# The FFN's up projection with high and low activations as one 512-column operand

## The chip, the cores and the metric

One core of a Trainium2 chip runs the kernel. The metric is the device time of one execution in microseconds (us), the median of several runs. Names: PE is TensorE's matmuls, PEld its weight loads, DVE is VectorE, ACT is ScalarE, POOL is GpSimd, SP is SyncE.

## What is computed

One decoder layer on 256 tokens of width 2048, in float32: a hybrid mixer, a cross-attention into 256 memory tokens, and an FFN, each with an RMSNorm before and after and a residual sum. The part that matters here is the FFN (width 5632, so 11,264 columns in the up projection), whose conv runs over the tokens:

```python
def conv_ffn(h, w_up, conv_w, conv_b, w_down):
    s = h.shape[1]
    up = h @ w_up
    up_pad = jnp.pad(up, ((0, 0), (CONV_WIDTH - 1, 0), (0, 0)))
    conv = conv_b + sum(up_pad[:, j:j + s] * conv_w[j] for j in range(CONV_WIDTH))
    gate, val = jnp.split(conv, 2, axis=-1)
    return (jax.nn.gelu(gate, approximate=True) * val) @ w_down
```

## The kernel before

Every large product is made of three: operands are split into a high part (rounded to `fp32r`) and a low part (the rest), and high x high, high x low and low x high are summed in PSUM. Weights come from memory in units of 512 KB (`raw_load`, line 204, four buffers), ScalarE casts the high half (line 220) and VectorE subtracts it from the raw weights for the low half (line 222), each with three buffers (`split`, line 214).

In `wstat` (line 241) the weights are the stationary operand and the activations stream as 256 columns, one for each token. A call makes 256 output columns, that is two weight tiles of 128 (`t`), in two PSUM tiles `mm` of which only the first 256 of 512 columns are used; four such tiles turn. Its 16 k-tiles come as four units of four. For each unit and each `t` there are 12 matmuls: high weights with high and low activations alternately for four k-tiles (lines 252 and 254), then the low weights with the high activations for the four (line 257). Each matmul loads its weights anew. In `xstat` the activations are stationary and the weights stream as 512 columns (lines 277, 279, 283); the down projection uses that.

The FFN runs 22 steps of two `wstat` calls, gate columns and value columns (lines 1392 and 1397), 44 calls and 88 weight tiles in all. Behind a call, `conv` (line 1380) takes each of the two PSUM tiles: VectorE multiplies by the tokens' norm factor `x2row` (1382) into `z`, ScalarE makes the first conv term with the bias (1383), VectorE adds the two shifted terms (1384, 1386). Behind the gate there is a GELU (1395); behind the value the product of both (1400) and its split into `hid` (1403, 1404), which waits in SBUF for the down projection.

The activations `h3T` are made by `transposed` (line 333): PE transposes, ScalarE casts the high part, VectorE makes the low part (line 329). A `Packed` holder keeps a tile with the high parts of two k-tiles and another with their low parts. All 16 buffers `h` are taken by it; they come free during the last call, when the last gains are loaded into four of them from GpSimd's queue.

A scheduler sets the order of each engine's instructions from priorities. Casts and differences of the split are issued with a high priority (`AHEAD`), so that they stand ahead of the conv of calls that come earlier in the program text; on an engine instructions run in the order in which they stand.

Of the kernel before, what the change touches and what calls it, by code (L numbers as in the profile page):

```python
# [61 lines left out]
class Packed:  # L62


    def __init__(self, per):
        self.per = per
        self.hi = []
        self.lo = []
# [3 lines left out]

    def l(self, k):
        return self.lo[k // self.per][:, k % self.per, :]


class Concat:
# [82 lines left out]
def hybrid_block(tc, a, out, dbg=None):  # L160
    nc = tc.nc
    dbg = dbg or {}
    with ExitStack() as ctx:
# [17 lines left out]
        def view(t_, **kw):  # L181
            keys = " ".join(kw)
            return t_.rearrange(f"p ({keys}) -> p {keys}", **kw)
# [57 lines left out]
        def wstat(src, c0, nco, X, kts=None):  # L241
# [17 lines left out]
                    L.advance(UNIT * n / 8)  # L259
            return [p[:, :S] for p in ps]  # L260

        def xstat(src, kts, c0, nco, X, ps, first=True, last=True, tail=1):


            nk = len(kts)
            hold = []
            for k0, n, hv, lv in units(src, kts, c0, nco):
                hold.append((k0, n, hv, lv))
                if nk - tail * n <= k0 and k0 + n < nk:
                    continue  # L270
                for t in range(2):
                    ts_ = slice(t * P, (t + 1) * P)
                    o = ps[t][:, :nco]
                    for k0, n, hv, lv in hold:
                        for k in range(n):
                            kk = kts[k0 + k]
                            nc.tensor.matmul(o, lhsT=X.h(kk)[:, ts_], rhs=hv[:, k, :],  # L277
                                             start=(first and k0 + k == 0), stop=False)
                            nc.tensor.matmul(o, lhsT=X.l(kk)[:, ts_], rhs=hv[:, k, :],  # L279
                                             start=False, stop=False)  # L280
                        for k in range(n):
                            kk = kts[k0 + k]
                            L.last = nc.tensor.matmul(o, lhsT=X.h(kk)[:, ts_], rhs=lv[:, k, :],  # L283
                                                      start=False, stop=(last and k0 + k == nk - 1))
                        L.advance(UNIT * n * nco / 2048)
                hold = []
# [43 lines left out]
                                               op1=ALU.subtract)  # L330
            return r

        def transposed(X, src, gcol, new):


            for j in range(KT // 2):
                ps = (auxp, auxq)[j % 2]()
                pv = view(ps, k=2, t=S)
                for t in range(2):
                    for k in range(2):  # L340
                        f = (2 * j + k) * P
                        nc.tensor.transpose(pv[:, k, t * P:(t + 1) * P],
                                            src[t][f // 512][:, f % 512:f % 512 + P], ident)
                hi = view(new(), k=2, t=S)
                lo = view(new(), k=2, t=S)
                for k in range(2):
                    X.last = put_hi_lo(hi[:, k, :], lo[:, k, :], pv[:, k, :], scale=gcol(2 * j + k))
                X.hi.append(hi)
                X.lo.append(lo)
                yield 1.5  # L350

        def row_factors(src, tmp, pins=(None,) * 4):
# [66 lines left out]
        def gcol(n):  # L419
            return lambda k: gpar[:, n * KT + k:n * KT + k + 1]  # L420
# [944 lines left out]
                    nc.sync.dma_start(dbg["x2"][t * P:(t + 1) * P, c * 512:(c + 1) * 512], x2[t][c])  # L1365


        h3T = Packed(2)
        with tc.high_priority(offset=2 * AHEAD):
            for _ in transposed(h3T, x2, gcol(2), hbuf):  # L1370
                pass
        x2row = over_rows(row_factors(x2, xtmp))
        right2.close()
# [5 lines left out]

        def conv(ps, dst, n):  # L1380
            z = mk(fp, "z", 4, (P, S))
            nc.vector.tensor_tensor(z, ps, x2row, op=ALU.mult)  # L1382
            nc.scalar.activation(dst, z, AF.Identity, bias=cw[:, 3, n:n + 1], scale=cw[:, 2, n:n + 1])  # L1383
            nc.vector.scalar_tensor_tensor(dst[:, 1:], z[:, :S - 1], cw[:, 1, n:n + 1], dst[:, 1:],  # L1384
                                           op0=ALU.mult, op1=ALU.add)
            nc.vector.scalar_tensor_tensor(dst[:, 2:], z[:, :S - 2], cw[:, 0, n:n + 1], dst[:, 2:],
                                           op0=ALU.mult, op1=ALU.add)

        hid = Packed(2)
        for j in range(FT // 2):  # L1390
            g = mk(fp, "gv", 4)
            ps = wstat(w_up, j * 256, 256, h3T)
            for t in range(2):
                conv(ps[t], g[:, t * S:(t + 1) * S], 2 * j + t)
            nc.scalar.activation(g, g, AF.Gelu_apprx_tanh)
            v = mk(fp, "gv", 4)
            ps = wstat(w_up, D_FF + j * 256, 256, h3T)
            for t in range(2):
                conv(ps[t], v[:, t * S:(t + 1) * S], FT + 2 * j + t)
            nc.vector.tensor_tensor(v, v, g, op=ALU.mult)  # L1400
            hi = mk(fp, "hid", FT, dt=F32R)
            lo = mk(fp, "hid", FT, dt=F32R)
            nc.scalar.copy(hi, v)
            nc.vector.tensor_tensor(lo, v, hi.bitcast(F32), op=ALU.subtract)
            hid.hi.append(view(hi, k=2, t=S))
            hid.lo.append(view(lo, k=2, t=S))
# [35 lines left out]
```

## Time and profile before

| | us |
|---|---|
| median of 3 runs | 1379.72 (1379.4 to 1380.31) |
| the profiled execution | 1382.32 |
| its span, first to last instruction | 1380.6 |
| PE busy | 1346.1 |
| PEld busy | 1250.1 |
| DVE busy | 867.5 |
| ACT busy | 685.1 |
| POOL busy | 78.7 |

The span is what the profile's views cover. The up projection lies at about 618 to 1132 us in it, the down projection behind that to about 1371 us. Ends of matmuls are modelled, and one begins while the one before it drains; so the distance of starts tells the pace, and the mean duration does not.

### The profile page before, as it was taken

Reading aid. Unit: us, or ns where it says so; the run is one execution under the profiler, and the core shown is the slowest. Engines: PE = TensorE matmul, PEld = TensorE weight load, DVE = VectorE, ACT = ScalarE, POOL = GpSimd, SP = SyncE. Lnnn points to the kernel's source line nnn. Section 1 sums busy time; section 2 is a strip of 40 time slices with the busy share of each in tenths; the row PEclk is TensorE's granted clock in tenths of the full one; section 3 lists DMA queues with packets and bytes.
Section 4 is the critical chain, followed back from the end, with each engine's and each line's share of the span. In section 5 each row is a group of like instructions: output and inputs, shape, how many; then the busy total and the mean of one; then the engine's idle time right before and its main releaser. Section 6 shows DMA issues by size and latency. Waiting matters only on the chain.

```text
span 1380.6 us, 23271 instructions
## 1 busy us (share of the span) xinstructions
PE 1346.1 (97%) x9412; PEld 1250.1 (91%) x9412; DVE 867.5 (63%) x1277; ACT 685.1 (50%) x1011; POOL 78.7 (6%) x99
## 2 busy tenths in 40 slices
PE   6999999999999999989999999999999999999997
PEld 6889989989988879869999999999999998888886
DVE  5679954456565765576666666666666674444444
ACT  6755372244456655566555555555555553434342
POOL 3011001120003110010000000000000000000001
PEclk9999999999999999999999999999999999999998
DMA  7545553145548755444655565555565566666663
GB/s 231 157 124 168 146 168 90 49 154 152 151 140 288 249 164 172 157 130 147 187 179 184 182 187 179 186 180 187 180 186 180 187 210 197 194 193 194 194 193 130
DMA packets 189849, 238.97 MB, mean 173 GB/s; under 512 B 7920, under 2 KB 144013, under 8 KB 189741
## 3 DMA queue, kind: packets, MB, share of 16 engines
q1 hardware_dynamic: 185802, 225.76, 53.0%
q0 software_dynamic: 3376, 11.29, 2.5%
q8 instruction: 74, 1.21, 0.4%
q10 hardware_dynamic: 563, 0.43, 0.1%
q14 instruction: 34, 0.28, 0.1%
HBM read 235.33 MB, written 2.12 MB: 172 GB/s over the span
## 4 chain that ended last, share of the span: by engine, by line
issue 57%; PE 37%; DVE 2%; POOL 1%; DMA 1%; ACT 1%; ACTq 0%; DVEq 0%; POOLq 0%
PE mm L252 5%; PE mm L257 5%; PE mm L254 5%; PE mm L277 4%; PE mm L279 4%; PE mm L283 4%; PE auxq L625 1%; DMA wa<-in_rwkv_w_up_dram 1%; PE auxq L742 1%; PE auxp L742 1%; DVE lo L222 1%; DMA raw<-in_w_in_dram 0%; PE auxq L864 0%; PE auxp L921 0%; PE auxp L892 0%
## 5 line engine op out<-in xcount | busy, mean ns | idle before, releaser
L222 DVE TENSOR_TENSOR lo<-raw,hi 128x1024 fp32r<-128x1024 f32 x422 | 516.6, 1225 | 373.5 <-ACT hi L220 372.1
L220 ACT CAST hi<-raw 128x1024 fp32r<-128x1024 f32 x422 | 441.8, 1048 | 459.1 <-PE mm L254 251.4
L252 PE MATMUL mm<-h,hi 128*128 128x256 f32 x2000 | 507.8, 286 | 1.6 <-ACT h L328 1.6
L254 PE MATMUL mm<-h,hi 128*128 128x256 f32 x2000 | 504.9, 285 | 0.3 <-DVE h L329 0.3
L252 PEld LDWEIGHTS mm<-h,hi 128*128 128x128 f32 x2000 | 385.2, 193 | 3.7 <-ACT h L328 1.8
L254 PEld LDWEIGHTS mm<-h,hi 128*128 128x128 f32 x2000 | 384.8, 193 | 1.3 <-DVE h L329 0.6
L257 PE MATMUL mm<-h,lo 128*128 128x256 f32 x2000 | 324.6, 284 | 0.0
L257 PEld LDWEIGHTS mm<-h,lo 128*128 128x128 f32 x2000 | 277.6, 193 | 1.2 <-issue 1.0
L279 PE MATMUL mm<-hi,hid 128*128 128x512 f32 x352 | 136.9, 389 | 0.0
L277 PE MATMUL mm<-hi,hid 128*128 128x512 f32 x352 | 136.9, 389 | 0.0
L283 PE MATMUL mm<-lo,hid 128*128 128x512 f32 x352 | 108.3, 389 | 0.0
L1383 ACT ACTIVATE gv<-z,cw 128x256 f32<-128x256 f32 x88 | 53.0, 602 | 71.6 <-DVE z L1382 71.6
L277 PE MATMUL mm<-hi,h 128*128 128x512 f32 (+1 forms) x208 | 78.9, 385 | 0.7 <-ACT hi L220 0.7
L277 PEld LDWEIGHTS mm<-hi,hid 128*128 128x128 f32 x352 | 66.1, 188 | 13.8
L283 PEld LDWEIGHTS mm<-lo,hid 128*128 128x128 f32 x352 | 66.1, 188 | 13.7
L279 PEld LDWEIGHTS mm<-hi,hid 128*128 128x128 f32 x352 | 66.0, 188 | 13.6
L279 PE MATMUL mm<-hi,h 128*128 128x512 f32 (+1 forms) x208 | 77.0, 375 | 0.0
L1384 DVE SCALAR_TENSOR_TENSOR gv<-z,cw,gv 128x255 f32<-128x255 f32 x88 | 42.3, 481 | 29.5 <-ACT gv L1383 29.5
L283 PE MATMUL mm<-lo,h 128*128 128x512 f32 (+1 forms) x208 | 59.6, 374 | 0.2 <-DVE lo L222 0.2
L277 PEld LDWEIGHTS mm<-hi,h 128*128 128x128 f32 x208 | 39.2, 188 | 8.1 <-ACT hi L220 1.1
L279 PEld LDWEIGHTS mm<-hi,h 128*128 128x128 f32 x208 | 39.2, 189 | 6.2
L283 PEld LDWEIGHTS mm<-lo,h 128*128 128x128 f32 x208 | 37.3, 188 | 7.7 <-DVE lo L222 0.8
(329 smaller groups left out, 1280.4 us busy)
## 6 DMA issues: line engine op xcount, KB each, us to landing
raw<-in_ffn_w_up_dram SPq DMA_DIRECT2D x176, 512.0 KB, 3.6
raw<-in_w_in_dram SPq DMA_DIRECT2D x94, 512.0 KB, 4.4
raw<-in_ffn_w_down_dram SPq DMA_DIRECT2D x88, 512.0 KB, 4.9
raw<-in_w_out_dram SPq DMA_DIRECT2D x32, 512.0 KB, 3.9
raw<-in_mem_wkv_dram SPq DMA_DIRECT2D x16, 512.0 KB, 4.2
raw<-in_mem_wq_dram SPq DMA_DIRECT2D x8, 512.0 KB, 3.6
raw<-in_mem_wo_dram SPq DMA_DIRECT2D x8, 512.0 KB, 3.7
x<-in_x_dram SPq DMA_DIRECT2D x8, 256.0 KB, 6.5
```

Of the source, the lines that this page charges most:

```text
L220: nc.scalar.copy(hv, rv)
L222: nc.vector.tensor_tensor(lv, rv, hv.bitcast(F32), op=ALU.subtract)
L252: nc.tensor.matmul(o, lhsT=hv[:, k, cs], rhs=X.h(k0 + k), start=(k0 + k == 0), stop=False)
L254: nc.tensor.matmul(o, lhsT=hv[:, k, cs], rhs=X.l(k0 + k), start=False, stop=False)
L257: L.last = nc.tensor.matmul(o, lhsT=lv[:, k, cs], rhs=X.h(k0 + k), start=False, stop=(k0 + k == nk - 1))
L277: nc.tensor.matmul(o, lhsT=X.h(kk)[:, ts_], rhs=hv[:, k, :], start=(first and k0 + k == 0), stop=False)
L279: nc.tensor.matmul(o, lhsT=X.l(kk)[:, ts_], rhs=hv[:, k, :], start=False, stop=False)
L283: L.last = nc.tensor.matmul(o, lhsT=X.h(kk)[:, ts_], rhs=lv[:, k, :], start=False, stop=(last and k0 + k == nk - 1))
L625: nc.tensor.matmul(ps[e][:, n * P:(n + 1) * P], lhsT=l[pr, t0:t0 + P], rhs=r[pr, t0:t0 + P], start=True, stop=True)
L742: nc.tensor.matmul(pv[:, n, c0:], lhsT=BN[:, g * 4 + n, :], rhs=G[g][:, n, c0:], start=True, stop=True)
L1383: nc.scalar.activation(dst, z, AF.Identity, bias=cw[:, 3, n:n + 1], scale=cw[:, 2, n:n + 1])
L1384: nc.vector.scalar_tensor_tensor(dst[:, 1:], z[:, :S - 1], cw[:, 1, n:n + 1], dst[:, 1:], op0=ALU.mult, op1=ALU.add)
```

## The change

The activations of the FFN lie in a new holder, `Paired`: for each k-tile one tile, whose first 256 columns are the high and whose last 256 are the low part. A new function, `wstat2`, makes one matmul of 512 columns with the high weights against that whole tile, into all 512 columns of the PSUM tile: the first half collects high x high, the second high x low. Directly behind it comes the matmul of the low weights with the 256 high columns, into the second half. `conv` then has two halves to add: ScalarE copies the second half to SBUF, VectorE adds the first half to it, and GpSimd multiplies by `x2row`. The first gate call keeps `wstat`; the other 43 calls use `wstat2`.

```diff
+class Paired:
+    def __init__(self):
+        self.hl = []
+    def h(self, k):
+        return self.hl[k][:, 0, :]
+    def l(self, k):
+        return self.hl[k][:, 1, :]
...
+        def wstat2(src, c0, nco, X):
+            nt = nco // P
+            ps = [mmps() for _ in range(nt)]
+            for k0, n, hv, lv in units(src, list(range(KT)), c0, nco):
+                for t in range(nt):
+                    cs = slice(t * P, (t + 1) * P)
+                    for k in range(n):
+                        nc.tensor.matmul(view(ps[t], z=2, t=S), lhsT=hv[:, k, cs], rhs=X.hl[k0 + k],
+                                         start=(k0 + k == 0), stop=False)
+                        L.last = nc.tensor.matmul(ps[t][:, S:], lhsT=lv[:, k, cs], rhs=X.h(k0 + k),
+                                                  start=False, stop=(k0 + k == KT - 1))
+                    L.advance(UNIT * n / 8)
+            return ps
...
-                hi = view(new(), k=2, t=S)
-                lo = view(new(), k=2, t=S)
+                one, two = view(new(), k=2, t=S), view(new(), k=2, t=S)
                 for k in range(2):
-                    X.last = put_hi_lo(hi[:, k, :], lo[:, k, :], pv[:, k, :], scale=gcol(2 * j + k))
...
+                    hi, lo = ((one, two)[k][:, i, :] if paired else (one, two)[i][:, k, :] for i in range(2))
+                    X.last = put_hi_lo(hi, lo, pv[:, k, :], scale=gcol(2 * j + k))
+                if paired:
+                    X.hl += [one, two]
...
-        h3T = Packed(2)
+        h3T = Paired()
...
         def conv(ps, dst, n):
             z = mk(fp, "z", 4, (P, S))
-            nc.vector.tensor_tensor(z, ps, x2row, op=ALU.mult)
+            if ps.shape[1] == S:
+                nc.vector.tensor_tensor(z, ps, x2row, op=ALU.mult)
+            else:
+                nc.scalar.copy(z, ps[:, S:])
+                nc.vector.tensor_tensor(z, ps[:, :S], z, op=ALU.add)
+                nc.gpsimd.tensor_tensor(z, z, x2row, op=ALU.mult)
...
-            ps = wstat(w_up, j * 256, 256, h3T)
+            ps = (wstat2 if j else wstat)(w_up, j * 256, 256, h3T)
...
-            ps = wstat(w_up, D_FF + j * 256, 256, h3T)
+            ps = wstat2(w_up, D_FF + j * 256, 256, h3T)
```

The order on PE, for one unit and one weight tile in the middle of the up projection (`mm` is the PSUM tile, `h` activations, `hi` and `lo` the weights' halves; a number is a buffer's own). Before:

```order
L252 MATMUL mm_9934<-h_6326,hi_9998 128x256
L254 MATMUL mm_9934<-h_6327,hi_9998 128x256
L252 MATMUL mm_9934<-h_6326,hi_9998 128x256
L254 MATMUL mm_9934<-h_6327,hi_9998 128x256
L252 MATMUL mm_9934<-h_6337,hi_9998 128x256
L254 MATMUL mm_9934<-h_6338,hi_9998 128x256
L252 MATMUL mm_9934<-h_6337,hi_9998 128x256
L254 MATMUL mm_9934<-h_6338,hi_9998 128x256
L257 MATMUL mm_9934<-h_6326,lo_9999 128x256 x2
L257 MATMUL mm_9934<-h_6337,lo_9999 128x256 x2
```

and with the change:

```order
L284 MATMUL mm_8044<-h_6326,hi_8092 128x512
L286 MATMUL mm_8044<-h_6326,lo_8093 128x256
L284 MATMUL mm_8044<-h_6327,hi_8092 128x512
L286 MATMUL mm_8044<-h_6327,lo_8093 128x256
L284 MATMUL mm_8044<-h_6337,hi_8092 128x512
L286 MATMUL mm_8044<-h_6337,lo_8093 128x256
L284 MATMUL mm_8044<-h_6338,hi_8092 128x512
L286 MATMUL mm_8044<-h_6338,lo_8093 128x256
```

Twelve matmuls of 256 columns are now eight, four of 512 and four of 256, and the low weights come second instead of ninth.

The order on ACT behind a value call. Before:

```order
L1383 ACTIVATE gv_8979<-z_9102,cw 128x256
L220 CAST hi_9182<-raw_9180 128x1024
L1383 ACTIVATE gv_8979<-z_9107,cw 128x256
L220 CAST hi_9212<-raw_9210 128x1024
L1403 CAST hid_9113<-gv_8979 128x512
L220 CAST hi_9256<-raw_9254 128x1024
L220 CAST hi_9286<-raw_9284 128x1024
```

and with the change:

```order
L1417 COPY z_8134<-mm_8044 128x256
L233 CAST hi_8202<-raw_8200 128x1024
L1420 ACTIVATE gv_8043<-z_8134,cw 128x256
L1417 COPY z_8141<-mm_8045 128x256
L233 CAST hi_8224<-raw_8222 128x1024
L1420 ACTIVATE gv_8043<-z_8141,cw 128x256
L233 CAST hi_8264<-raw_8262 128x1024
L1440 CAST hid_8149<-gv_8043 128x512
L233 CAST hi_8286<-raw_8284 128x1024
```

A copy of the low half stands ahead of each `gv` step, the first of them ahead of the cast that was behind the step.

The order on DVE behind a value call, from its first `z` to the next call's. Before:

```order
L1382 TENSOR_TENSOR z_9646<-mm_9524,rrow_6390 128x256
L1384 SCALAR_TENSOR_TENSOR gv_9523<-z_9646,cw,gv_9523 128x255
L1382 TENSOR_TENSOR z_9651<-mm_9525,rrow_6390 128x256
L1386 SCALAR_TENSOR_TENSOR gv_9523<-z_9646,cw,gv_9523 128x254
L222 TENSOR_TENSOR lo_9727<-raw_9724,hi_9726 128x1024
L1384 SCALAR_TENSOR_TENSOR gv_9523<-z_9651,cw,gv_9523 128x255
L1386 SCALAR_TENSOR_TENSOR gv_9523<-z_9651,cw,gv_9523 128x254
L1400 TENSOR_TENSOR gv_9523<-gv_9523,gv_9389 128x512
L222 TENSOR_TENSOR lo_9757<-raw_9754,hi_9756 128x1024
L1404 TENSOR_TENSOR hid_9658<-gv_9523,hid_9657 128x512
L222 TENSOR_TENSOR lo_9801<-raw_9798,hi_9800 128x1024
```

and with the change:

```order
L1418 TENSOR_TENSOR z_8134<-mm_8044,z_8134 128x256
L235 TENSOR_TENSOR lo_8203<-raw_8200,hi_8202 128x1024
L1421 SCALAR_TENSOR_TENSOR gv_8043<-z_8134,cw,gv_8043 128x255
L1418 TENSOR_TENSOR z_8141<-mm_8045,z_8141 128x256
L1423 SCALAR_TENSOR_TENSOR gv_8043<-z_8134,cw,gv_8043 128x254
L235 TENSOR_TENSOR lo_8225<-raw_8222,hi_8224 128x1024
L1421 SCALAR_TENSOR_TENSOR gv_8043<-z_8141,cw,gv_8043 128x255
L1423 SCALAR_TENSOR_TENSOR gv_8043<-z_8141,cw,gv_8043 128x254
L1437 TENSOR_TENSOR gv_8043<-gv_8043,gv_7937 128x512
L235 TENSOR_TENSOR lo_8265<-raw_8262,hi_8264 128x1024
L1441 TENSOR_TENSOR hid_8150<-gv_8043,hid_8149 128x512
L235 TENSOR_TENSOR lo_8287<-raw_8284,hi_8286 128x1024
```

The sum of the two halves stands where the product by the norm factor stood; the first low difference, which stood behind two shifted conv terms, now stands ahead of them.

## Rows read from the trace of the kernel before

**Rows 1.** The page, parts 1 and 2: busy time, share of the span and instructions of each engine, and the granted TensorE clock in 40 slices, in tenths.

```profile
PE 1346.1 (97%) x9412; PEld 1250.1 (91%) x9412; DVE 867.5 (63%) x1277; ACT 685.1 (50%) x1011; POOL 78.7 (6%) x99
...
PEclk9999999999999999999999999999999999999998
```

**Rows 2.** Busy time by stretches (us from the span's start): the start of the up projection, its middle, and the down projection. Columns: stretch, length, busy us (count) of PE, PEld, DVE, ACT and POOL, granted clock, share of the DMA engines, GB/s.

```profile
620.00:630.00 10.00, 9.69 (x60) 9.42 (x60) 7.36 (x16) 8.35 (x24) 0.00 (x0) 0.69 0.17 54
660.00:1120.00 460.00, 460.00 (x3835) 460.00 (x3835) 313.19 (x440) 231.56 (x279) 0.00 (x0) 1.00 0.59 184
1150.00:1300.00 150.00, 150.00 (x663) 124.21 (x662) 70.36 (x60) 60.56 (x63) 0.00 (x0) 1.00 0.63 193
```

**Rows 3.** The waits from 690 to 1130 us, the two longest that lie in the way of the splits: who waited for whom, us in total, times, longest.

```profile
ACT hi L220 <- PE mm L254: 145.6, 114, 1.8
DVE lo L222 <- ACT hi L220: 115.9, 97, 1.7
```

**Rows 4.** The instructions of line 257, the low weights' matmul, from 654.85 to 1130.05 us: count, duration in ns (least, median, most), first and last start.

```profile
L257 PE MATMUL mm<-h,lo x1320: 283/283/284, 654.9 to 1129.0; 128*128 128x256 f32 x189
```

**Rows 5.** The timeline of PE, the first burst of that count and the first one behind it: start in us, us from the first start to the last end, engine, line, operation, how many.

```profile
654.90 0.64 PE L257 MATMUL mm<-h,lo 128*128 128x256 f32 x4
...
1130.10 0.64 PE L257 MATMUL mm<-h,lo 128*128 128x256 f32 x4
```

**Rows 6.** The timeline of PE in the down projection, columns as in the group before.

```profile
1201.41 0.39 PE L277 MATMUL mm<-hi,hid 128*128 128x512 f32 x1
1201.63 0.39 PE L279 MATMUL mm<-hi,hid 128*128 128x512 f32 x1
1201.86 0.39 PE L277 MATMUL mm<-hi,hid 128*128 128x512 f32 x1
1202.09 0.39 PE L279 MATMUL mm<-hi,hid 128*128 128x512 f32 x1
1202.31 0.61 PE L283 MATMUL mm<-lo,hid 128*128 128x512 f32 x2
1202.77 0.39 PE L277 MATMUL mm<-hi,hid 128*128 128x512 f32 x1
```

**Rows 7.** The timeline of PE at the two passages between sizes: from the mixer's gate (512 columns) to its next projection (256), and from the up to the down projection.

```profile
325.80 0.62 PE L283 MATMUL mm<-lo,h 128*128 128x512 f32 x2
326.25 0.28 PE L252 MATMUL mm<-h,hi 128*128 128x256 f32 x1
...
1131.54 0.64 PE L257 MATMUL mm<-h,lo 128*128 128x256 f32 x4
1132.02 0.40 PE L277 MATMUL mm<-hi,hid 128*128 128x512 f32 x1
```

**Rows 8.** The timeline around the end of one unit of the up projection; in brackets the idle time before and what ended it.

```profile
806.10 0.64 PE L257 MATMUL mm<-h,lo 128*128 128x256 f32 x4
806.30 1.05 ACT L220 CAST hi<-raw 128x1024 fp32r<-128x1024 f32 x1 [1.83 <-PE mm L254]
807.38 1.23 DVE L222 TENSOR_TENSOR lo<-raw,hi 128x1024 fp32r<-128x1024 f32 x1 [1.65 <-ACT hi L220]
```

**Rows 9.** Instructions by line and shape, 690 to 1130 us: line, engine, operation, out<-in, count, busy us, mean ns of one, idle time before them and what ended it.

```profile
L222 DVE TENSOR_TENSOR lo<-raw,hi 128x1024 fp32r<-128x1024 f32 x154 | 188.3, 1223 | 115.9 <-ACT hi L220 115.9
L220 ACT CAST hi<-raw 128x1024 fp32r<-128x1024 f32 x153 | 159.8, 1044 | 147.0 <-PE mm L254 145.6 <-PE mm L257 1.3
L1383 ACT ACTIVATE gv<-z,cw 128x256 f32<-128x256 f32 x76 | 45.7, 602 | 61.8 <-DVE z L1382 61.8
L1384 DVE SCALAR_TENSOR_TENSOR gv<-z,cw,gv 128x255 f32<-128x255 f32 x76 | 36.5, 481 | 25.4 <-ACT gv L1383 25.4
L1386 DVE SCALAR_TENSOR_TENSOR gv<-z,cw,gv 128x254 f32<-128x254 f32 x76 | 36.4, 479 | 1.3
L1382 DVE TENSOR_TENSOR z<-mm,rrow 128x256 f32<-128x256 f32 x76 | 31.7, 417 | 0.0
L1400 DVE TENSOR_TENSOR gv<-gv,gv 128x512 f32<-128x512 f32 x19 | 13.2, 693 | 0.7
L1404 DVE TENSOR_TENSOR hid<-gv,hid 128x512 fp32r<-128x512 f32 x19 | 13.0, 684 | 0.0
```

**Rows 10.** The instructions of line 867, a ScalarE copy from PSUM in the mixer; columns as in rows 4.

```profile
L867 ACT COPY s<-auxq x6: 372/372/378, 246.1 to 278.6; 128x256 f32<-128x256 f32 x6
```

**Rows 11.** What GpSimd and VectorE do beside each other elsewhere, by the views of single lines; columns as in rows 4. Lines 1264 and 1266 are the two halves of a residual sum and run at the same time.

```profile
L806 POOL TENSOR_TENSOR nat<-nat,wa x3: 1346/1349/1446, 136.2 to 175.6; 128x512 f32<-128x512 f32 x3
...
L1264 POOL TENSOR_TENSOR yg<-yg,row x2: 1758/1759/1760, 503.1 to 511.0; 128x512 f32<-128x512 f32 x2
...
L1266 DVE SCALAR_TENSOR_TENSOR yg<-yg,small,row x6: 743/751/1773, 502.3 to 511.5; 128x512 f32<-128x512 f32 x6
...
L436 POOL MEMSET cmask<- x1: 312/312/312, 0.9 to 0.9; 128x256 f32 x1
...
L568 POOL MEMSET v<- x1: 527/527/527, 41.5 to 41.5; 128x516 f32 x1
```

**Rows 12.** The page, part 6: the up projection's loads, KB each, median us from issue to landing.

```profile
raw<-in_ffn_w_up_dram SPq DMA_DIRECT2D x176, 512.0 KB, 3.6
```

**Rows 13.** The timeline of PE at the start of the up projection.

```profile
616.66 0.69 PE L342 MATMUL auxp<-ident,row 128*128 128x128 f32 x2 [3.40 <-DVE row L1266]
618.28 0.78 PE L252 MATMUL mm<-h,hi 128*128 128x256 f32 x2
```

More of the change, by code (lines that the diff above doesn't have):

```diff
@@ L331, in put_hi_lo, with transposed @@
             return r
-        def transposed(X, src, gcol, new):
+        def transposed(X, src, gcol, new, paired=False):
             for j in range(KT // 2):
@@ L343, in transposed @@
                                             src[t][f // 512][:, f % 512:f % 512 + P], ident)
-                hi = view(new(), k=2, t=S)
-                lo = view(new(), k=2, t=S)
+                one, two = view(new(), k=2, t=S), view(new(), k=2, t=S)
                 for k in range(2):
-                    X.last = put_hi_lo(hi[:, k, :], lo[:, k, :], pv[:, k, :], scale=gcol(2 * j + k))
-                X.hi.append(hi)
-                X.lo.append(lo)
+                    hi, lo = ((one, two)[k][:, i, :] if paired else (one, two)[i][:, k, :] for i in range(2))
[3 more added lines that the diff above has]
+                else:
+                    X.hi.append(one)
+                    X.lo.append(two)
                 yield 1.5
@@ L1365, in hybrid_block @@
                     nc.sync.dma_start(dbg["x2"][t * P:(t + 1) * P, c * 512:(c + 1) * 512], x2[t][c])
-        h3T = Packed(2)
+        h3T = Paired()
         with tc.high_priority(offset=2 * AHEAD):
-            for _ in transposed(h3T, x2, gcol(2), hbuf):
+            for _ in transposed(h3T, x2, gcol(2), hbuf, paired=True):
                 pass
@@ L1381, in conv @@
             z = mk(fp, "z", 4, (P, S))
-            nc.vector.tensor_tensor(z, ps, x2row, op=ALU.mult)
+            if ps.shape[1] == S:
+                nc.vector.tensor_tensor(z, ps, x2row, op=ALU.mult)
+            else:
+                nc.scalar.copy(z, ps[:, S:])
+                nc.vector.tensor_tensor(z, ps[:, :S], z, op=ALU.add)
+                nc.gpsimd.tensor_tensor(z, z, x2row, op=ALU.mult)
             nc.scalar.activation(dst, z, AF.Identity, bias=cw[:, 3, n:n + 1], scale=cw[:, 2, n:n + 1])
```

## The prediction

> **What bounds the kernel now.** I read the busy shares first. TensorE is busy 97% of the span, VectorE 63%, ScalarE 50%, GpSimd 6%, and the granted clock is full in nearly every slice [rows 1]. A busy PE is no proof of a bound, because its ends are modelled, so I read the stage by stretches next: through the up projection (660 to 1120 us) PE and its weight loads are busy without a gap, VectorE is busy 313 of 460 us, ScalarE 232, GpSimd 0, and the clock is 1.00 [rows 2]. The waits say the same from the other side: ScalarE's high casts wait for PE 114 times, VectorE's low differences wait for ScalarE 97 times, and of this stage no wait of PE stands in the list [rows 3]. So PE's issue pace sets the time of this stage, and the splits run up to three buffers ahead of it.
>
> The pace comes from starts, not from durations. From the low burst at 654.90 us to the one at 1130.10 us [rows 5] lie 1,320 low matmuls, four to a burst [rows 4], so 330 bursts of 12 matmuls: 475.20 / 330 = 1.440 us a burst, **120.0 ns for a matmul of 256 columns**, its weight load included. In the down projection six matmuls of 512 columns start between 1201.41 and 1202.77 us [rows 6]: **226.7 ns each**. Their difference, 106.7 ns, is 256 columns at 2.4 GHz; what is left of both, 13.3 ns, is a cost per matmul that does not grow with its columns. That is what the change can save.
>
> **The change part by part.** *Matmuls.* For one k-tile and one weight tile there were three matmuls of 256 columns, 3 x 120.0 = 360.0 ns; now one of 512 and one of 256, 226.7 + 120.0 = 346.7 ns. 13.3 ns go. 43 of the 44 calls are changed (the diff leaves the first as it was), each with 2 weight tiles and 16 k-tiles: 1,376 pairs, 1,376 x 13.33 ns = **18.3 us**. The streamed columns stay 768. Sizes mixed in one stream are not in the trace in steady state, but both passages are: the last 256-column matmul of a burst of four at 1131.54 us and the first of 512 behind it lie 120 ns apart (1131.54 + 4 x 0.12 = 1132.02), and two 512-column matmuls from 325.80 us with a 256-column one behind them at 326.25 us take 0.225 us each [rows 7]. Neither passage pays extra. Bounds: nothing saved, if the mixed stream kept 360 ns, and 26.7 ns a pair (36.7 us), if a second fixed cost also vanished. I take 13.3, which is where both passages lie. Is the clock in danger when columns are denser? The down projection, with 512 of every 544 cycles used, holds 1.00 [rows 2].
>
> The rows say 13.3 ns of fixed cost per matmul. The Trainium skill, page "TensorE: Matmul & The Clock Gate", section "Back-to-back issue gap", gives about 2.5 ns beside the columns when the clock is full; by that, 1,376 matmuls fewer would be worth an estimated 3.4 us, and the median would come to 1376.3 us. For the sum the measurement decides; what could keep the cost where it is stands among the rivals.
>
> *Low weights earlier.* A unit of four k-tiles used its low half a third of the way in; now at its second matmul. And high buffers, released at 20 of 24 matmuls before (the cast at 806.30 us starts while the last low burst from 806.10 us still runs, and the low difference follows at 807.38 us for 1.23 us [rows 8]), now come free only at the end. Three buffers turn, so the low half is needed two units after the release, 2 x 2.77 = 5.5 us, and costs a cast, 1.05, and a difference, 1.22 [rows 9]: some 3.2 us to spare when nothing stands between.
>
> *The conversion behind a call.* Before: one product from PSUM (0.42 us), the ScalarE step (0.60), two VectorE steps (0.48 each) [rows 9]. Now: a ScalarE copy from PSUM, 0.37 us by the nearest row [rows 10]; a VectorE sum from PSUM and SBUF, the old product's shape, 0.42; a GpSimd product of 128x256, which has no row. GpSimd's 128x512 tensor-tensor takes 1.35 us at the median of one line and 1.76 in another, where VectorE works beside it [rows 11], so 0.67 to 0.88 if it goes by columns, and 1.76 at most; I take 0.7 to 0.9, since its memsets do go by columns (0.31 us for 256, 0.53 for 516 [rows 11]). Per pair of calls VectorE is busy 8 x 1.22 + 4 x (0.42 + 0.48 + 0.48) + 0.69 + 0.68 = 16.7 us [rows 9], the same as before, of now 64 x 0.3467 = 22.2 us. ScalarE gets 4 x 0.37 us more.
>
> Does the longer chain hold back a split? I walk the order shown, from T, where PE ends a call's first tile. Copy to T+0.4, sum to 0.8, product to 1.6. The unit ends at 1.4: cast to 2.4, ScalarE step to 3.0, second copy to 3.4. VectorE: low difference 2.4 to 3.7, step to 4.1, second sum to 4.6, step to 5.0. The second product, held by that step, runs 5.0 to 5.8. ScalarE: cast at the next release, 4.2 to 5.2, step 5.8 to 6.4, free before the release at 6.9. VectorE may wait for GpSimd until 5.8: low difference to 7.0, two steps and the product of the halves to 8.6, low difference to 9.9, and so on to 12.0, after which the next call's sum follows without a backlog. The four low halves are ready at 3.7, 7.0, 9.9 and 12.0 and needed at 6.9, 9.7, 12.5 and 15.2: **at least 2.6 us to spare**. All of it lies beside PE and costs nothing; without that cover the copy and the product alone, 0.37 + 0.8 us for each of 86 tiles, would be 100 us.
>
> *Queues.* SP's order of loads is unchanged. Loads of 512 KB land in 3.6 us [rows 12]; 184 GB/s becomes 191, below the 193 the down projection draws without a gap [rows 2]. On GpSimd two gain loads now stand ahead of one product in the second last call; they wait for the first buffers of the last call, free at about T+3.5, and that product's input is ready at T+4.6. The PSUM tiles are released by VectorE's sum at T+4.6 instead of T+2, a call of 11.1 us before they are needed.
>
> *The start.* The up projection runs from 618.28 us to 1132.02 us [rows 7, 13], 513.7 us against 44 calls x 8 bursts x 1.44 = 506.9: it loses 6.9 us while activations are transposed and the clock is down to 0.69 [rows 2]. The pairs change in which tile a high and a low part lie, and with it the order there. Twelve matmuls, one burst, is the size by which that order moves: -1.5 to +2 us; I take 0.
>
> **Sum.** 18.3 us. The profiled execution took 1382.3 us (span 1380.6), 2.6 over the median 1379.7; all of it falls off the span: 1382.3 - 18.3 = 1364.0 for such an execution, 1379.7 - 18.3 = **1361.4 us** for the median.
>
> **The rivals.** *A lock (slower).* GpSimd and VectorE hold each other up: the VectorE step of 128x512 beside GpSimd's sum has a median of 751 ns and a maximum of 1773, and GpSimd's sum grows from 1.35 to 1.76 [rows 11]. Each of the four products in two calls takes VectorE's time if it blocks it whole, and VectorE becomes the bound from (22.2 - 16.7) / 4 = 1.37 us each on; a queue that is in order would suffer somewhat earlier. At 1.76 us: 16.7 + 7.0 = 23.7 us for two calls instead of 23.0 before, 21.5 times: +15 us, 1395 us. Against it: half the columns. 0.05. (The Trainium skill, page "SBUF — State Buffer", section "Who interferes with whom", states such an exclusive lock for a VectorE instruction with two SBUF inputs, which the low difference is; the maximum above agrees.)
>
> *Part of it eaten.* Products near 1.1 us make the step behind them late for some casts, or the start loses more than 2 us: 3 to 13 us faster, 1367 to 1377 us. 0.08.
>
> *The cost stays.* If the 13 ns go with the columns or with how closely a short matmul follows its weights, and not with the number of matmuls, a pair of unlike lengths keeps its 360 ns: no change, 1380 us. Against it: proportional to columns, 512 would take 240 ns and not 226.7, and both passages. 0.04. (The Trainium skill's figure above lies beside this case.) *A new wait of the same size*, a few tenths of a microsecond at each call's end, 18.3 / 43 = 0.43 us: 1380 us as well. Against it: 2.6 us to spare. 0.02.
>
> **How the numbers follow.** The forecast, 1359 to 1367 us, has 0.81. The range is that: 18.3 us with the start (-1.5 to +2) and 0.9 us of spread of the runs shown at the fast end, and 3.6 us of lost casts at the slow end; past it lies 0.19. About 0.2% (2.8 us) can be told from no change: faster 0.81 + 0.08 = 0.89, same 0.04 + 0.02 = 0.06, slower 0.05.
>
> **What would show it.** The two matmuls of a pair starting 0.347 us apart from the next pair; PE still without a gap between 660 us and the stage's end, which moves from 1132 to about 1114; VectorE's busy time nearly unchanged; 86 products on GpSimd of 0.7 to 0.9 us. It is wrong if PE waits for VectorE's low difference, if products take over 1.1 us, or if pairs stand more than 0.35 us apart.

## The result

The changed kernel takes 1373.83 us (median of 13 runs, 1371.59 to 1379.02), the kernel before 1380.98 us in the same comparison (13 runs, 1379.33 to 1384.02): a ratio of 0.9946, 95% interval 0.9936 to 0.9957. On the 1379.72 us shown above that is 1372.3 us. It is faster, by 7.4 us (5.9 to 8.8), where 18.3 us were forecast; the time lies above the range.

The profiled execution took 1375.61 us, its span is 1373.9 us. The page, parts 1 and 2, answers to [rows 1]:

```profile
PE 1337.0 (97%) x8036; PEld 1175.1 (86%) x8036; DVE 869.4 (63%) x1277; ACT 715.7 (52%) x1097; POOL 149.6 (11%) x185
...
PEclk9999999999999999999999999999999999999999
```

1,376 matmuls are gone (9,412 to 8,036), GpSimd has 86 instructions more, and VectorE's busy time is the old one. The stretches of [rows 2], columns as there:

```profile
660.00:1120.00 460.00, 460.00 (x2605) 398.95 (x2604) 320.13 (x449) 264.67 (x368) 69.60 (x86) 1.00 0.60 187
1150.00:1300.00 150.00, 150.00 (x663) 124.23 (x662) 69.95 (x59) 60.97 (x64) 0.00 (x0) 1.00 0.61 193
```

PE still has no gap, the clock is still 1.00, the loads draw 187 GB/s, fewer than the down projection's 193. The waits from 690 to 1110 us, as in [rows 3] (waiting line, line waited for, us in total, times, longest):

```profile
POOL z L1419 <- DVE z L1418: 357.4, 74, 7.2
ACT hi L233 <- PE mm L284: 150.9, 149, 1.3
DVE lo L235 <- ACT hi L233: 126.2, 130, 1.6
...
ACT gv L1420 <- POOL z L1419: 6.8, 37, 0.2
```

No wait of PE stands there, and the splits still wait for PE and not the other way round. The conversion steps by line and shape, 660 to 1100 us, answer to [rows 9, 10]:

```profile
L1419 POOL TENSOR_TENSOR z<-z,rrow 128x256 f32<-128x256 f32 x78 | 64.3, 824 | 376.6 <-DVE z L1418 376.6
...
L1418 DVE TENSOR_TENSOR z<-mm,z 128x256 f32<-128x256 f32 x78 | 32.5, 417 | 0.0
L1417 ACT COPY z<-mm 128x256 f32<-128x256 f32 x78 | 28.3, 362 | 18.8 <-PE mm L286 18.8
```

So everything beside PE went as forecast, and the time must be in PE's own stream. Its timeline in the middle of the stage (start in us, us from start to end, engine, line, how many):

```profile
799.72 0.40 PE L284 MATMUL mm<-h,hi 128*128 128x512 f32 x1
799.96 0.28 PE L286 MATMUL mm<-h,lo 128*128 128x256 f32 x1
800.07 0.40 PE L284 MATMUL mm<-h,hi 128*128 128x512 f32 x1
...
805.37 0.40 PE L284 MATMUL mm<-h,hi 128*128 128x512 f32 x1
```

From 799.72 to 805.37 us lie 16 pairs: **353.3 ns a pair** (mean over the stage), where the bare prices add up to 346.7. The one of 512 columns takes some 236 ns to the next start, the one of 256 some 117. The stage from its first matmul to the first of the down projection, which answers to [rows 7, 13]:

```profile
621.09 0.78 PE L265 MATMUL mm<-h,hi 128*128 128x256 f32 x2
...
1125.49 0.40 PE L306 MATMUL mm<-hi,hid 128*128 128x512 f32 x1
```

504.4 us, 9.3 less than the 513.7 before, and 1,376 x (360.0 - 353.3) = 9.2. The stage's remainder is the old one: 504.4 - 1,376 x 0.3533 - 32 x 0.36 (the first call) = 6.7 us, 6.9 before. PE's gain is thus 6.7 ns a pair instead of 13.3.

### The profile page after: what moved, and what is told of

The parts are those of the page before. It is cut to its first block, busy times and chain, and to the rows that moved or that the text cites. A ratio compares the mean times of both kernels' runs of the same rounds, so it can differ in the third digit from the quotient of the medians.

```text
span 1373.9 us, 20692 instructions
## 1 busy us (share of the span) xinstructions
PE 1337.0 (97%) x8036; PEld 1175.1 (86%) x8036; DVE 869.4 (63%) x1277; ACT 715.7 (52%) x1097; POOL 149.6 (11%) x185
## 4 chain that ended last, share of the span: by engine, by line
PE 91%; issue 3%; DVE 2%; DMA 1%; ACT 1%; POOL 1%; ACTq 0%; DVEq 0%; POOLq 0%
PE mm L284 24%; PE mm L286 12%; PE mm L306 10%; PE mm L308 10%; PE mm L312 10%; PE mm L265 6%; PE mm L270 5%; PE mm L267 5%; PE auxq L657 1%; DMA wa<-in_rwkv_w_up_dram 1%; DVE lo L235 1%; PE auxq L774 1%; PE auxp L774 1%; DMA raw<-in_w_in_dram 0%; ACT hi L233 0%
## 5 line engine op out<-in xcount | busy, mean ns | idle before, releaser
L284 PE MATMUL mm<-h,hi 128*128 128x512 f32 x1376 | 486.3, 399 | 0.0
L286 PE MATMUL mm<-h,lo 128*128 128x256 f32 x1376 | 386.5, 281 | 0.0
L284 PEld LDWEIGHTS mm<-h,hi 128*128 128x128 f32 x1376 | 258.6, 188 | 64.4
L286 PEld LDWEIGHTS mm<-h,lo 128*128 128x128 f32 x1376 | 260.0, 189 | 0.0
L265 PE MATMUL mm<-h,hi 128*128 128x256 f32 x624 | 162.6, 293 | 2.0 <-ACT h L357 2.0
L267 PE MATMUL mm<-h,hi 128*128 128x256 f32 x624 | 160.2, 288 | 0.7 <-DVE h L358 0.7
L265 PEld LDWEIGHTS mm<-h,hi 128*128 128x128 f32 x624 | 120.8, 195 | 4.3 <-ACT h L357 2.2
L267 PEld LDWEIGHTS mm<-h,hi 128*128 128x128 f32 x624 | 120.6, 194 | 1.7 <-DVE h L358 1.0
L1419 POOL TENSOR_TENSOR z<-z,rrow 128x256 f32<-128x256 f32 x86 | 70.7, 822 | 427.5 <-DVE z L1418 427.5
L270 PE MATMUL mm<-h,lo 128*128 128x256 f32 x624 | 102.5, 286 | 0.0
L270 PEld LDWEIGHTS mm<-h,lo 128*128 128x128 f32 x624 | 87.2, 193 | 1.3 <-issue 1.0
```

Source lines behind the costliest of these rows:

```text
L265: nc.tensor.matmul(o, lhsT=hv[:, k, cs], rhs=X.h(k0 + k), start=(k0 + k == 0), stop=False)
L267: nc.tensor.matmul(o, lhsT=hv[:, k, cs], rhs=X.l(k0 + k), start=False, stop=False)
L270: L.last = nc.tensor.matmul(o, lhsT=lv[:, k, cs], rhs=X.h(k0 + k), start=False, stop=(k0 + k == nk - 1))
L284: nc.tensor.matmul(view(ps[t], z=2, t=S), lhsT=hv[:, k, cs], rhs=X.hl[k0 + k], start=(k0 + k == 0), stop=False)
L286: L.last = nc.tensor.matmul(ps[t][:, S:], lhsT=lv[:, k, cs], rhs=X.h(k0 + k), start=False, stop=(k0 + k == KT - 1))
L1419: nc.gpsimd.tensor_tensor(z, z, x2row, op=ALU.mult)
```

## The experiments

All are edits of the changed kernel, in `wstat2`. "Stage" is the distance from the first matmul of line 265 to the first one on `hid`. Times without a spread are from a single execution; those of the groups of four and of eight are medians of six.

### Which part of the change costs

**Three matmuls of 256 in the new order, with everything else of the change kept.**

```diff
-    nc.tensor.matmul(view(ps[t], z=2, t=S), lhsT=hv[:, k, cs], rhs=X.hl[k0 + k],
+    nc.tensor.matmul(ps[t][:, :S], lhsT=hv[:, k, cs], rhs=X.h(k0 + k),
                      start=(k0 + k == 0), stop=False)
+    nc.tensor.matmul(ps[t][:, S:], lhsT=hv[:, k, cs], rhs=X.l(k0 + k),
+                     start=False, stop=False)
```

> The change with one edit: the 512-column matmul is split into two of 256 with the high weights, into the two halves, and the low weights' matmul follows directly as in the change. All lengths are equal, the weight tiles alternate. If the change of length costs the missing time, three matmuls take 3 x 120.0 = 360 ns and the up projection takes as long as before the change, 513.7 us. If low weights directly behind high ones cost it, they take 366.6 ns, 9 us more. It also shows alone what the conversion with a copy, a sum and a GpSimd product costs: nothing if the up projection takes 513.7 us.

Measured: 1381.01 us, stage 514.1 us, as before the change. On PE, ten groups of three:

```profile
799.86 0.28 PE L284 MATMUL mm<-h,hi 128*128 128x256 f32 x1
799.98 0.28 PE L286 MATMUL mm<-h,hi 128*128 128x256 f32 x1
800.10 0.28 PE L288 MATMUL mm<-h,lo 128*128 128x256 f32 x1
...
803.46 0.28 PE L284 MATMUL mm<-h,hi 128*128 128x256 f32 x1
```

3.60 us, 120.0 ns for each matmul. High and low weights in turn, the early low half, the new conversion and GpSimd's products cost next to nothing together (0.4 us over the 513.7 of before).

**The low weights on 512 columns too** (this adds the product of both low parts).

```diff
-    L.last = nc.tensor.matmul(ps[t][:, S:], lhsT=lv[:, k, cs], rhs=X.h(k0 + k),
+    L.last = nc.tensor.matmul(view(ps[t], z=2, t=S), lhsT=lv[:, k, cs], rhs=X.hl[k0 + k],
```

> The change with one edit: the low weights also meet the 512 columns (the product low x low is added, which the other kernels leave out), so that all matmuls have 512 columns and the weight tiles alternate. If the change of length costs the missing time, a pair takes 2 x 226.7 = 453.3 ns; if low weights directly behind high ones cost it, 460 ns. The up projection grows by 1,376 x 100 ns = 138 us from 504.4 us in the first case, by 147 us in the second.

Measured: 1514.73 us, stage 642.4 us. Ten pairs in 4.54 us:

```profile
799.93 0.39 PE L284 MATMUL mm<-h,hi 128*128 128x512 f32 x1
...
804.47 0.39 PE L284 MATMUL mm<-h,hi 128*128 128x512 f32 x1
```

453.3 ns a pair, 226.7 each. Neither the 512-column operand nor the turn of weights costs; what is left is that the two lengths stand side by side.

**The low product into the first half of the PSUM tile.**

```diff
-    L.last = nc.tensor.matmul(ps[t][:, S:], lhsT=lv[:, k, cs], rhs=X.h(k0 + k),
+    L.last = nc.tensor.matmul(ps[t][:, :S], lhsT=lv[:, k, cs], rhs=X.h(k0 + k),
```

> The change with one edit: the low weights' matmul adds into the first half of the PSUM tile instead of the second (the sum of the halves is the same). If the missing 6.6 ns come from writing the half that the 512-column matmul has just left, a pair takes 346.7 ns and the time falls by 9 us. If they come from the change of length, or from the change of weight tile, a pair stays at 353.3 ns.

Measured: 1373.76 us, stage 503.4 us, pairs 353.3 ns apart (ten from 799.62 to 803.16 us). Which half of the tile it writes is not the cause.

### Which lengths

Here only the columns differ; `x` is the 512-column tile, and the first k-tile of each output keeps 512 with the high weights. For 384 with 384:

```diff
-    nc.tensor.matmul(view(ps[t], z=2, t=S), lhsT=hv[:, k, cs], rhs=X.hl[k0 + k],
+    x = X.hl[k0 + k].rearrange("p z t -> p (z t)")
+    c = 384 if k0 + k else 512
+    nc.tensor.matmul(ps[t][:, :c], lhsT=hv[:, k, cs], rhs=x[:, :c],
...
-    L.last = nc.tensor.matmul(ps[t][:, S:], lhsT=lv[:, k, cs], rhs=X.h(k0 + k),
+    L.last = nc.tensor.matmul(ps[t][:, :384], lhsT=lv[:, k, cs], rhs=x[:, :384],
```

The others are the same edit with one of the two lengths left at 512 or 256, or with other numbers. High weights on fewer than 512 columns leave out part of their product with the low activations; low weights on more than 256 add part of a product of two low parts, and on 128 they leave out half of theirs.

**384 with 384.** 

> The change with the same 768 columns in two equal matmuls: high and low weights each meet the first 384 of the 512 columns (left out: high x low for half of the tokens from the second k-tile on; added: low x low for the others). If only unequal lengths keep the pair from 346.7 ns, as the runs with three of 256 (360.0) and two of 512 (453.3) say, the pair takes 2 x (160 + 13.3) = 346.7 ns, and the up projection 504.4 - 1,376 x 0.0066 = 495.3 us. If a second matmul costs more whenever its low weights follow directly and the row is shorter than 512, it stays near 353.

**512 with 384.** 

> The change with 384 instead of 256 columns behind the 512 (low x low is added for half of the tokens). Theory of the change of length: any two unequal lengths cost, the pair takes 226.7 + 173.3 + 6.6 = 406.6 ns. Rival, the cover: what costs is that a 256-column matmul, 106.7 ns of columns, just fails to cover the next weight load when the one before was longer; 384 columns cover it, and the pair takes 400.0 ns.

**512 with 128.** 

> The change with 128 instead of 256 columns behind the 512 (left out: low x high for half of the tokens). Theory of the change of length: the pair takes 226.7 + 66.7 + 6.6 = 300 ns. Rival, the cover: 128 columns, 53 ns, hide half of a load at most, so the next 512 starts late by what a load lacks: 226.7 + at least 95 (the interval at which 128-column transposes with a load each follow one another in the mixer) = 322 ns or more, up to 346 if a load takes the 120 ns of a 256-column matmul.

**Four of 128** (`x[:, :128]` and `x[:, 128:256]`, with the high and then with the low weights). 

> Each pair of the up projection becomes four matmuls of 128 columns, two with the high and two with the low weights (the product of the high weights with the low activations is left out), all of one length. Theory A (what costs is a change of length; a matmul in a run of its own length takes columns / 2.4 GHz plus 13.3 ns): 66.7 ns from start to start inside a unit, four take 266.7 ns. Theory C (each matmul with its weight load needs at least some 113 ns, which is what is left of the 340.0 ns of the pair of 512 and 128 columns once 226.7 are taken off): 113.3 ns each, four take 453.3 ns. If it is 66.7, the 47 ns that the pair of 512 and 128 pays over its two bare prices belong to the change of length; if it is over 100, most of them are a floor for short matmuls, and that pair says little on the change. Stage waits between units may come in, since conversion and loads have to keep up with 2.13 us a unit: only the distances inside a unit count.

**384 with 256.** 

> High weights on 384 columns (half of the product with the low activations is left out), low weights on 256. Bare prices 173.3 + 120.0 = 293.3 ns. Theory A (a change between any two lengths costs): 300.0 to 306.7 ns a pair, as 512 with 256 pays 6.7 and 512 with 384 pays 13.3. Theory D (only the 512-column form pays, when it has to get going after a shorter one): 293.3 ns. Theory C (a floor of some 113 ns for a short one): 293.3 ns too, both being above it. Stage end to end at 300.0: some 431 us.

**448 with 256.** 

> High weights on 448 columns (a quarter of the high weights' product with the activations is left out), low weights on 256. Bare: 448 / 2.4 + 13.3 = 200.0 ns, and 120.0 ns: 320.0 ns a pair. Theory D (only the form of 512 columns pays after a shorter one, as the pair of 384 and 256 cost its bare 293.3): 320.0. Theory E (what counts is how much longer the first of the two is: nothing at 128 columns more, 6.7 ns at 256 more): 322 to 327 ns. The stage at 320.0: some 459 us, or some 464 us with the first step's 512 columns in each output.

**512 with 448.** 

> High weights on 512 columns, low weights on 448. Bare 226.7 + 200.0 = 426.7 ns. Theory D (512 pays after any shorter one): 433 to 440 ns, as with 384, which paid 13.3. Theory E (the difference in length counts, and here it is 64 columns): 426.7 ns.

Measured, from start to start on PE, with columns / 2.4 GHz + 13.3 ns as the bare price:

| columns | bare, ns | measured, ns | more | time, us | stage, us |
|---|---|---|---|---|---|
| 256 + 256 + 256 | 360.0 | 360.0 | 0 | 1381.01 | 514.1 |
| 384 + 384 | 346.7 | 346.7 | 0 | 1374.21 | 500.2 |
| 512 + 512 | 453.3 | 453.3 | 0 | 1514.73 | 642.4 |
| 384 + 256 | 293.3 | 293.3 | 0 | 1309.25 | 438.3 |
| 448 + 256 | 320.0 | 320.0 | 0 | 1331.35 | 462.2 |
| 512 + 256 | 346.7 | 353.3 | 6.7 | 1373.83 | 504.4 |
| 512 + 384 | 400.0 | 413.3 | 13.3 | 1458.52 | 587.2 |
| 512 + 448 | 426.7 | 433.3 | 6.7 | 1483.84 | 612.9 |
| 512 + 128 | 293.3 | 340.0 | 46.7 | 1369.59 | 501.6 |
| 128 x 4 | 266.7 | 446.7 | 180 | 1509.59 | 642.5 |

The rows behind it, one kernel after the other: 384 with 384 (18 matmuls), 512 with 384, 384 with 256, 448 with 256, 512 with 448 (the first and the last start of 10, 12, 5 and 10 pairs):

```profile
800.86 0.33 PE L288 MATMUL mm<-h,lo 128*128 128x384 f32 x1
...
803.98 0.33 PE L288 MATMUL mm<-h,lo 128*128 128x384 f32 x1
```

```profile
799.57 0.40 PE L284 MATMUL mm<-h,hi 128*128 128x512 f32 x1
...
803.71 0.40 PE L284 MATMUL mm<-h,hi 128*128 128x512 f32 x1
```

```profile
796.25 0.34 PE L286 MATMUL mm<-h,hi 128*128 128x384 f32 x1
...
799.77 0.34 PE L286 MATMUL mm<-h,hi 128*128 128x384 f32 x1
```

```profile
759.71 0.36 PE L286 MATMUL mm<-h,hi 128*128 128x448 f32 x1
...
761.31 0.39 PE L286 MATMUL mm<-h,hi 128*128 128x512 f32 x1
```

```profile
759.64 0.39 PE L284 MATMUL mm<-h,hi 128*128 128x512 f32 x1
...
763.97 0.39 PE L284 MATMUL mm<-h,hi 128*128 128x512 f32 x1
```

and 512 with 128 (ten pairs) and the four of 128 (ten fours):

```profile
799.66 0.44 PE L284 MATMUL mm<-h,hi 128*128 128x512 f32 x1
799.94 0.22 PE L286 MATMUL mm<-h,lo 128*128 128x128 f32 x1
...
803.06 0.44 PE L284 MATMUL mm<-h,hi 128*128 128x512 f32 x1
```

```profile
799.76 0.27 PE L286 MATMUL mm<-h,hi 128*128 128x128 f32 x1
...
804.23 0.27 PE L286 MATMUL mm<-h,hi 128*128 128x128 f32 x1
```

Two things follow. Matmuls of 128 columns, each with its weight load, come only every 111.7 ns (446.7 / 4), so the pair with 128 says little on mixing: 226.7 + 111.7 is 338.4 of its 340.0. (The expectation for that pair reads 95 ns between 128-column transposes; in the traces of both kernels the closest stand 108 ns apart.) And it is not the change of length as such: 384 with 256 and 448 with 256 cost their bare price, so the theory that any change costs falls, and so does the one by the difference in length (512 with 448 pays, 384 with 256 does not). The cover falls too: 384 columns behind the 512 were to cover the next weight load and cost nothing, and they cost 13.3 ns. **In a steady alternation only the form of 512 columns pays, when a shorter one stands ahead of it**: with 256, 384 and 448. How much it pays (6.7, 13.3, 6.7) follows no rule that these runs show. Nor is the 512 alone in it where the pattern is broken: behind the one 512 that each output keeps, the pairs of 448 and 256 take 329, 325 and 316 ns before they are back at 320.

The one 512 of each output also lengthens the stages of the edits with 384 or 448 high columns (with 384 and 384 to 500.2 us from 1,376 x 0.3467 + 18.2 = 495.2, where 18.2 is the start and the first call of the changed kernel). But those of 512 with 128 and of 384 with 256 are longer still than their pairs make them (the first: 1,376 x 0.340 + 18.2 = 486.0 us, against 501.6). There PE does wait, and for the low difference; the waits of PE's weight loads, in the first of them from 660 to 1110 us and in the second to 1040 us:

```profile
PEld mm L286 <- DVE lo L235: 14.1, 20, 0.7
```

```profile
PEld mm L288 <- DVE lo L235: 13.2, 39, 0.4
```

The length of the pair alone does not decide where the cover ends, behind which the conversion lies: with 448 and 256, at 320.0 ns a pair, there is none of these waits, and PE has no gap (columns as in [rows 2]):

```profile
660.00:1050.00 390.00, 390.00 (x2421) 369.31 (x2420) 302.62 (x417) 245.70 (x340) 61.91 (x75) 1.00 0.66 204
```

With 512 and 128 the order on ScalarE is another. The `gv` step stands directly behind its copy, without a cast between them, and ScalarE waits there for GpSimd's product, 81 times from 660 to 1110 us, 179.9 us in all:

```profile
803.94 0.37 ACT L1417 COPY z<-mm 128x256 f32<-128x256 f32 x1
806.58 0.60 ACT L1420 ACTIVATE gv<-z,cw 128x256 f32<-128x256 f32 x1 [2.27 <-POOL z L1419]
```

With 384 and 256 the order is that of the change, but 85 of the 86 products meet a low difference, and the one that begins later is held up: 42 products that begin behind a low difference take 1.65 us on average instead of 0.74, and the 43 low differences that begin behind a product take 1.67 us instead of 1.22:

```profile
805.64 1.22 DVE L235 TENSOR_TENSOR lo<-raw,hi 128x1024 fp32r<-128x1024 f32 x1
...
809.32 1.68 DVE L235 TENSOR_TENSOR lo<-raw,hi 128x1024 fp32r<-128x1024 f32 x1
```

```profile
805.80 1.65 POOL L1421 TENSOR_TENSOR z<-z,rrow 128x256 f32<-128x256 f32 x1 [5.33 <-DVE z L1420]
809.01 0.91 POOL L1421 TENSOR_TENSOR z<-z,rrow 128x256 f32<-128x256 f32 x1 [1.57 <-DVE z L1420]
```

So in the order of the change the cover ends somewhere between 320 and 293 ns a pair. That these longer products and differences make the low halves late there fits the waits, but no run takes them away.

### How often the passage is paid

If it is the 512 behind a shorter one that pays, longer runs of one length should pay less often. Two, four (one weight tile of a unit) and eight (both tiles) of 512 columns stand ahead of as many of 256:

```diff
                     for k in range(n):
                         nc.tensor.matmul(view(ps[t], z=2, t=S), lhsT=hv[:, k, cs], rhs=X.hl[k0 + k],
                                          start=(k0 + k == 0), stop=False)
+                    for k in range(n):
                         L.last = nc.tensor.matmul(ps[t][:, S:], lhsT=lv[:, k, cs], rhs=X.h(k0 + k),
                                                   start=False, stop=(k0 + k == KT - 1))
```

That is the group of four. For eight the new loop is over `t` and `k`, behind the whole loop over `t`; for two both loops run over `(j, j + 1)` inside `for j in range(0, n, 2)`.

**Four.** 

> The change with one edit: for each unit and weight tile first the four 512-column matmuls of the high weights, then the four of 256 columns of the low weights, so two changes of length in a burst of eight instead of eight. In the changed kernel a pair takes 353.3 ns where 346.7 was forecast. If what is missing belongs to the alternation (of lengths, of PSUM halves or of weight tiles), a burst of four pairs takes 4 x 346.7 + 6.6 = 1393 ns instead of 1413, over 344 bursts 6.8 us less: about 1367 us by the median. If 512-column matmuls with the activations as the moving operand are slower in themselves, the burst stays at 1413 ns and the time at 1374 us.

**Eight.** 

> The change with the eight 512-column matmuls of a unit's two weight tiles first and its eight of 256 columns behind them: two changes of length in 16 matmuls. Grouping by four gave 1400 ns for four pairs, 13.3 over the sum. If a change up and down costs 13.3 ns however long the groups are, eight pairs take 8 x 346.7 + 13.3 = 2787 ns, against 2800 by fours and 2827 in the change: 172 x 0.040 = 6.9 us less than the change, the up projection 497.5 us and the time about 1368 us. If the cost grows with the groups, to the 20 ns that the passages of the kernel before show (26.7 up, 6.7 given back down), 2793 ns and 1 us more.

**Two.** 

> Two matmuls of 512 columns, then two of 256: bare 693.3 ns. One change each way per pair costs 6.7 ns in the changed kernel, 13.3 ns per four pairs in groups of four, 20 ns per eight in groups of eight. Theory A, with the cost of a change growing as the run behind it gets longer and levelling off: 700.0 to 706.7 ns per two pairs (350.0 to 353.3 a pair), so a stage of 500.5 to 504.5 us. A fixed price per change, whatever the length of the run, would have been 13.3 ns for the changed kernel's pair as well, and is out already; 693.3 would say that the first change is the only one that costs.

The timelines of four and of eight:

```profile
801.52 1.08 PE L284 MATMUL mm<-h,hi 128*128 128x512 f32 x4
802.45 0.64 PE L287 MATMUL mm<-h,lo 128*128 128x256 f32 x4
802.92 0.39 PE L284 MATMUL mm<-h,hi 128*128 128x512 f32 x1
```

```profile
798.88 2.00 PE L284 MATMUL mm<-h,hi 128*128 128x512 f32 x8
800.72 1.12 PE L289 MATMUL mm<-h,lo 128*128 128x256 f32 x8
801.67 2.00 PE L284 MATMUL mm<-h,hi 128*128 128x512 f32 x8
```

and of two, with 19 cycles between the rows:

```profile
800.02 0.62 PE L285 MATMUL mm<-h,hi 128*128 128x512 f32 x2
...
813.25 0.63 PE L285 MATMUL mm<-h,hi 128*128 128x512 f32 x2
```

| group | cycle, ns | more than bare | per pair, ns | stage, us | time, us | ratio to before |
|---|---|---|---|---|---|---|
| one (the change) | 353.3 | 6.7 | 353.3 | 504.4 | 1373.83 | 0.9946 (0.9936 to 0.9957) |
| two | 696.7 | 3.3 | 348.3 | 497.6 | 1370.59, one run | |
| four | 1400 | 13.3 | 350.0 | 500.3 | 1371.23 (1364.74 to 1372.67) | 0.9929 (0.9911 to 0.9946) |
| eight | 2793.3 | 20.0 | 349.2 | 499.0 | 1367.08 (1365.93 to 1369.46) | 0.9910 (0.9893 to 0.9926) |

In the cycle of eight the 512s pay: 798.88 to 800.72 us is 1.84 us for eight, 1.81 by 226.7 ns; the 256s give back some: 0.95 us, 0.96 by 120.0. Grouping by eight lies below the change with both intervals apart, and below the kernel before. It changes nothing but the order, which agrees with the passage as the cause. Of the two values expected by fours, 1,393 and 1,413 ns, neither came (1,400); by eights the 2,793 of a cost that grows with the groups came. The cost of a cycle does not simply grow with its length, though: two were to pay 6.7 to 13.3 ns and pay 3.3, less than one.

## Why the prediction was wrong

- **What bounds, and the cover: right.** PE has no gap from 660 us to the stage's end, the clock stays at 1.00, no split is late, VectorE's sum takes 417 ns and the copy 362 (0.42 and 0.37 forecast), the 86 products 0.82 us on average (0.7 to 0.9), none over 0.92. The kernel with three matmuls of 256 in the new order shows it as a whole: 514.1 us for the stage, 513.7 before.
- **The start: right.** 6.7 us are lost there, 6.9 before.
- **The two prices: right.** 384 with 384 and 448 with 256, which were in no row of before, fall on columns / 2.4 GHz + 13.3 ns as well. The Trainium skill, page "TensorE: Matmul & The Clock Gate", section "Back-to-back issue gap", gives 2.5 ns in place of the 13.3, but for a matmul by itself, without a budget for weight loads. The prediction's estimate by it leaves that condition out. For a stream of weight loads and matmuls the same section gives about 131 ns at 512 columns; these runs, with 226.7, do not agree with that either.
- **"Neither passage pays extra": wrong.** This is the step that failed, and with it the sum "226.7 + 120.0 = 346.7 ns". The pair pays 6.7 ns, half of what was to be saved: 1,376 x 6.7 = 9.2 of the 18.3 us. The rows were there. [rows 7] gives only the start of the first 512-column matmul, which tells what the last 256 took, and nothing on the 512 behind it. The same view from the next row on:

```profile
1132.25 0.40 PE L279 MATMUL mm<-hi,hid 128*128 128x512 f32 x1
1132.49 0.39 PE L277 MATMUL mm<-hi,hid 128*128 128x512 f32 x1
...
1133.41 0.39 PE L277 MATMUL mm<-hi,hid 128*128 128x512 f32 x1
```

  From the first start in [rows 7], 1132.02 us, six matmuls of 512 columns take 1.39 us, where six take 1.36 in [rows 6]: some 27 ns more. That is the passage, and the group of eight pays it each time (28 ns on its 512s, 20 with what the 256s give back). The lower price in [rows 6] is that of a stream which has long settled, and the prediction took it for the price of any 512. Paid in full at each pair it would have made the change slower (366.7 ns); the true pair lies between. The sign that the text named for this, pairs more than 0.35 us apart, is what the timeline shows.
- **The rivals.** The time fell where "part of it eaten" put it (1367 to 1377 us), but by another mechanism: no product is near 1.1 us and the start loses nothing. The mechanism is nearer to "the cost stays", which spoke of pairs of unlike lengths: half of the 13.3 ns stays. "Against it: both passages" was the same misreading. The lock did not come, but not because the columns are half as many: of the 86 products 43 meet no instruction of VectorE at all and take 0.74 us, and 43 meet a conv step, for 0.31 us on average, and the begin of a low difference, for 0.13, and take 0.91. The view of their line (count, least, median, most in ns):

```profile
L1419 POOL TENSOR_TENSOR z<-z,rrow x86: 732/751/916, 650.7 to 1128.7; 128x256 f32<-128x256 f32 x86
```

  Where a product begins behind a low difference, with 384 and 256, its 1.65 us come near the rival's 1.76. In the changed kernel the products run at other times, and none begins behind a low difference that still runs.
- **The range** held the bounds "0 to 26.7 ns a pair" in the text but was built around 13.3 alone; the price of a mixed stream, which no row showed in steady state and on which the whole sum rests, had 4% in one rival. That the change is faster at all is therefore in part luck: paid in full, the passage would have turned the sign.
- **Open.** Timed, the change gains 7.4 us, the stage of the profiled executions 9.3; the part before the stage is the difference: it ends at 618.28 us in the one profile of before and at 616.6 to 623.9 us in the 14 of the changed kernel and its edits, 620.2 on average. Whether the change shifts it or the one profile of before came out short there can't be told from these runs. Open is also why 512 columns pay and 448 don't: what in the engine differs was not measured.

## What to carry to other kernels

Merging two matmuls into one saves the fixed cost of one, here 13.3 ns, but a price read in a long uniform stream holds only in such a stream: before mixing lengths, read in the trace what the first several matmuls behind a passage take, not only where the first one starts. Where lengths must mix, their order is part of the price: the same matmuls grouped by unit take 349.2 ns a pair instead of 353.3, and gain 12 us instead of 7 on the kernel before. Look also how far the cover of what stands beside the stream reaches: it depends on the order of the other engines and on what runs beside what, and not on the stream's pace alone.

## What the runs showed of the hardware

- Matmuls of 128 columns of this type, each with its own weight load, come every 111.7 ns in a stream of them (53.3 ns by columns); no two 128-column transposes in the kernel before or the changed one start closer than 108 ns.
- The fixed 13.3 ns holds for 256, 384 and 512 columns in a stream of one length, and for the sum of a pair where 384 or 448 columns alternate with 256. 512 columns alternating with 256, 384 or 448 take on average 231 to 238 ns from start to start instead of 226.7, and behind a run of 256 they settle only some five matmuls on.
- The modelled durations show it in small: 512 columns last 0.39 us when settled and 0.40 in the changed kernel (mean 399 ns on line 284, 389 on line 308).
- GpSimd's product of 128x256 takes 0.74 us with VectorE idle. Where it and a low difference meet, with 384 and 256, the one that begins first keeps its time (low difference 1.22 us, product 0.90) and the other grows (product to 1.65 us, low difference to 1.67, on average).
